# A two-layer diffusion backbone on one Trainium2 core: smaller position table, start normalization per modulation set, output projection in two token parts

## The chip, the cores and the metric

The kernel runs on one core of one Trainium2 chip. The metric is device microseconds of one launch. Five instruction streams matter: PE (TensorE; PEld are its weight loads), DVE (VectorE), ACT (ScalarE), POOL (GpSimd), and SP, which only issues DMAs. Each runs its own list in order and waits for others by semaphores.

## The reference, cut to what matters

640 tokens of 1024 channels go through two layers: 512 latent tokens with a position embedding added, and 128 context tokens. Each group has its own shift, scale and gate, from a small product with `w_mod`.

```python
er = r[:, None] * omega                 # r = t // 64, 8 values
ec = col[:, None] * omega               # col = t % 64, 64 values
pos = concatenate([sin(er), cos(er), sin(ec), cos(ec)], -1)
...
h = rmsnorm(x, norm_g) * (1.0 + scale) + shift
z = h @ w_in                            # feeds three mixers: Hyena, S5, gated DeltaNet
...
merged = sum(gates * proj)              # one projection and gate per mixer
x = x + gate * (merged @ w_out)         # output projection, residual
```

After two layers there is one last `rmsnorm`.

## The kernel before, in words

Activations lie channels on partitions, tokens along the row: `x` is eight tiles `xs[k]` of [128 channels, 640 tokens], tokens 0 to 511 latent, 512 to 639 context. For a float32-like product each operand is split in a high and a low half by `split`: ACT copies the rounded high half (L69), DVE or POOL subtracts for the low half (L70). `mm3` (L91) then makes three matmuls for each of 8 channel blocks. `proj` makes one output tile: two weight pieces of 4 blocks (`kh` 0, 1), each used for token slices 0:320 and 320:640, so 48 matmuls of 320 columns.

`start` loads `x` (tiles `xi`), the full position table (two tiles of 1 MB) and layer 0's modulation weights (four sets `wm`, 2 MB each). It transposes `x` on PE, adds the table (L271), sums squares (`square_acc`), then runs `mod_set` four times. Set `s` gives shift and scale for channel blocks `s` and `4+s`. `norm_h` stands behind all of it: `rstd` becomes a row over all partitions (`dg`, two matmuls with ones L352 and L353, `rs`), and for each of eight blocks `k` it multiplies (`xn`, L359), applies scale and shift (`hf`, L362), and splits into `hh` and `hl`.

Then in each layer: the S5 mixer and Hyena interleaved, the DeltaNet, and `merge`. The 40 gate tiles (`gates`, PSUM name `pg`) are projections that nobody needs until `merge`, 48 matmuls each; in the program they are free to stand between the mixers' own matmuls. `merge` ends with the output projection: for each of eight tiles `i` a full `proj` of all 640 tokens (operands `mh`, `ml`), the gated residual (L132), square and sum (L323, L324). After the last tile come `rstd` (PE L333, DVE `rsv`, POOL L338) and the next layer's `norm_h`, or `final`, which transposes `x` back, scales and stores.

The order of instructions within each engine is not written by hand: a list scheduler with a model of time places them when the program is built, so an edit anywhere can move rows everywhere. Line numbers here are those of the kernel before. In the rows of the changed program most of them are shifted: L90 is the matmul of `mm3`, L131 the residual, L330 and L333 the squares, L334 their sum, L344 to L350 `rstd`, L365 and L366 the ones-matmul and `rs`, L374 `xn`, L378 `hf`, L296 `mrow`.

## Time and profile before

| | |
|---|---|
| median of 3 runs | 3660.12 us (3655.4 to 3660.27) |
| profiled execution, device time | 3638.89 us |
| span of its instructions | 3637.1 us |
| PE busy | 3347.8 us (92%) |
| DVE busy | 2371.0 us (65%) |
| POOL busy | 1948.5 us (54%) |
| ACT busy | 1414.8 us (39%) |
| mean granted TensorE clock | 0.958 |

PE is the engine that is nearly always at work; the other engines have room on the whole, but not in every stage. [...]

### The profile page before, as it was taken

What the parts mean: (1) busy time and instruction counts of PE and PEld (TensorE: products, weight loads), DVE (VectorE), ACT (ScalarE), POOL (GpSimd) and SP (SyncE); (2) the same over time, 40 slices, a digit from 0 to 9 for tenths busy, and PEclk for the clock granted to TensorE, in tenths of its full rate; (3) what the DMA queues carried; (4) which work ended last, traced back from release to release, by engine and by line L of the source; (5) the groups of instructions that cost most, each with busy time, mean ns of one, the idle gap of its engine ahead of it and who ended that gap; (6) DMA issues with size and microseconds to landing.
All of it is one profiled execution on the core that took longest, in us unless ns stands there. A gap on an engine that the chain in (4) does not pass through costs nothing.

```text
span 3637.1 us, 68480 instructions
## 1 busy us (share of the span) xinstructions
PE 3347.8 (92%) x25850; PEld 3198.3 (88%) x25850; DVE 2371.0 (65%) x4615; ACT 1414.8 (39%) x3295; POOL 1948.5 (54%) x2153
## 2 busy tenths in 40 slices
PE   6899988899999999899979999999999999899998
PEld 5898877799899999899968888988898998898998
DVE  5767677667537876743747776677773378875354
ACT  4433322233254556353334333333322545555422
POOL 3887777668545444301336778787774454351010
PEclk7899988899999999999989999999999999899999
DMA  6322334322232222543623222233222322134352
GB/s 238 122 64 77 88 109 140 96 69 78 74 100 75 68 70 86 169 135 112 196 99 101 73 76 85 75 79 81 77 61 74 107 69 77 46 104 166 111 182 87
DMA packets 294195, 363.04 MB, mean 100 GB/s; under 512 B 86792, under 2 KB 169768, under 8 KB 293610
## 3 DMA queue, kind: packets, MB, share of 16 engines
q1 hardware_dynamic: 282050, 342.15, 30.7%
q10 hardware_dynamic: 11816, 16.53, 1.6%
q8 instruction: 204, 3.34, 0.4%
q14 instruction: 125, 1.02, 0.1%
HBM read 291.87 MB, written 66.67 MB: 99 GB/s over the span
## 4 chain that ended last, share of the span: by engine, by line
PE 47%; DVE 18%; POOL 11%; issue 8%; DMA 3%; ACT 2%; SPq 1%; POOLq 0%; DVEq 0%; ACTq 0%
PE pj L91 21%; PE pg L91 10%; DVE lt L1334 2%; DVE Yl L1335 2%; PE pb L129 1%; POOL Y L669 1%; POOL et L830 1%; POOL wl L70 1%; PE pb L659 1%; PE pb L661 1%; POOL E L829 1%; DVE R L939 1%; PE pb L997 1%; PE pb L908 1%; POOL E L831 1%
## 5 line engine op out<-in xcount | busy, mean ns | idle before, releaser
L91 PE MATMUL pj<-hh,wh 128*128 128x320 f32 x2048 | 656.4, 321 | 28.3 <-ACT hh L69 17.6
L91 PE MATMUL pj<-hl,wh 128*128 128x320 f32 x2048 | 652.9, 319 | 5.6 <-DVE hl L70 5.5
L91 PE MATMUL pj<-hh,wl 128*128 128x320 f32 x2048 | 649.9, 318 | 2.4 <-POOL wl L70 2.2
L69 ACT CAST wh<-wr 128x512 fp32r<-128x512 f32 x608 | 374.8, 618 | 662.1 <-PE pj L91 515.2
L70 POOL TENSOR_TENSOR wl<-wr,wh 128x512 fp32r<-128x512 f32 x288 | 394.2, 1372 | 380.9 <-ACT wh L69 340.8
L91 PEld LDWEIGHTS pj<-hh,wh 128*128 128x128 f32 x2048 | 393.4, 192 | 37.0 <-ACT hh L69 19.8
L91 PE MATMUL pg<-hh,wh 128*128 128x320 f32 x1280 | 417.7, 327 | 7.0 <-ACT gst L1423 3.4
L70 DVE TENSOR_TENSOR wl<-wr,wh 128x512 fp32r<-128x512 f32 x320 | 252.5, 791 | 253.9 <-ACT wh L69 252.4
L91 PE MATMUL pg<-hh,wl 128*128 128x320 f32 x1280 | 411.6, 326 | 6.0 <-POOL wl L70 6.0
L91 PE MATMUL pg<-hl,wh 128*128 128x320 f32 x1280 | 412.3, 323 | 0.0
L91 PEld LDWEIGHTS pj<-hl,wh 128*128 128x128 f32 x2048 | 393.1, 192 | 11.1 <-DVE hl L70 8.8
L91 PEld LDWEIGHTS pj<-hh,wl 128*128 128x128 f32 x2048 | 392.4, 192 | 5.9 <-POOL wl L70 3.5
L91 PE MATMUL pj<-yl,wh 128*128 128x320 f32 x1024 | 318.0, 311 | 2.5 <-DVE yl L70 2.2
L91 PE MATMUL pj<-yh,wh 128*128 128x320 f32 x1024 | 317.0, 312 | 2.0 <-ACT yh L69 1.2
L91 PE MATMUL pj<-yh,wl 128*128 128x320 f32 x1024 | 316.9, 310 | 0.0
L91 PEld LDWEIGHTS pg<-hh,wh 128*128 128x128 f32 x1280 | 252.4, 197 | 9.8 <-ACT wh L69 5.3
L91 PEld LDWEIGHTS pg<-hh,wl 128*128 128x128 f32 x1280 | 249.1, 196 | 10.7 <-POOL wl L70 9.2
L91 PEld LDWEIGHTS pg<-hl,wh 128*128 128x128 f32 x1280 | 252.0, 197 | 0.9 <-issue 0.4
L91 PEld LDWEIGHTS pj<-yl,wh 128*128 128x128 f32 x1024 | 193.2, 189 | 4.0 <-DVE yl L70 4.0
L91 PEld LDWEIGHTS pj<-yh,wh 128*128 128x128 f32 x1024 | 192.6, 189 | 3.5 <-ACT yh L69 2.2
L91 PEld LDWEIGHTS pj<-yh,wl 128*128 128x128 f32 x1024 | 193.1, 189 | 0.0
L1513 POOL TENSOR_TENSOR m<-m,gt 128x640 f32<-128x640 f32 x16 | 31.1, 1943 | 294.4 <-DVE gt L132 294.4
(523 smaller groups left out, 8675.9 us busy)
## 6 DMA issues: line engine op xcount, KB each, us to landing
wr<-in_wt SPq DMA_DIRECT2D x608, 256.0 KB, 2.8
gt<-gst SPq DMA_DIRECT2D x160, 160.0 KB, 2.0
gt<-gt SPq DMA_DIRECT2D x64, 320.0 KB, 3.3
wr<-in_wmod SPq DMA_DIRECT2D x64, 256.0 KB, 3.1
Pm<-gcd ACTq DMA_DIRECT2D x32, 320.0 KB, 3.7
wm<-in_wmod SPq DMA_DIRECT2D x4, 2048.0 KB, 18.8
M<-ks SPq DMA_DIRECT2D x256, 32.0 KB, 1.8
us<-u ACTq DMA_DIRECT2D x16, 328.0 KB, 3.2
```

Of the source, the lines that this page charges most:

```text
L69: self.nc.scalar.copy(h, src)
L70: (eng or self.nc.vector).tensor_tensor(l, src, h.bitcast(F32), op=ALU.subtract)
L91: ins = self.nc.tensor.matmul(o, w[:, k, :m], x[:, kh * 4 + k, s], start=kh == 0 and k == 0 and i == 0, stop=kh == 1 and k == 3 and i == 2)
L129: self.nc.tensor.transpose(out, in_, self.ident[:k, :k])
L659: nc.tensor.matmul(pv[:, f, 0, :], D[mr][:, k, j], z[:, k, xr, :], start=k == 0, stop=k == 1)
L661: nc.tensor.matmul(pv[:, f, 1, :], D[mi][:, k, j], z[:, k, xi, :], start=k == 0, stop=k == 1)
L669: nc.gpsimd.tensor_tensor(Y[:, fs, 0, :], p1[:, :nf, 0, :], p2[:, :nf, 0, :], op=ALU.subtract)
L829: nc.gpsimd.tensor_tensor(E[:, 0:2, :, d], E[:, 0:2, :, s], bc(E[:, 0:1, :, e:e + 1], sh), op=ALU.mult)
L830: nc.gpsimd.tensor_tensor(t, E[:, ::-1, :, s], bc(m, sh), op=ALU.mult)
L831: nc.gpsimd.tensor_tensor(E[:, 0:2, :, d], E[:, 0:2, :, d], t, op=ALU.add)
L1334: nc.vector.tensor_tensor(tv, bc(LL[:, c:c + 1, 0:c], sh), bc(Y[:, c:32, c:c + 1], sh), op=ALU.mult)
L1335: nc.vector.tensor_tensor(Y[:, c:32, 0:c], Y[:, c:32, 0:c], tv, op=ALU.subtract)
```

## The change

Four edits. (1) The position table holds 8 row values and 64 column values (288 numbers a partition, 0.15 MB) and is broadcast in the add. (2) In `start` the ones-matmuls and `rs` come before the modulation sets, and after each set the two channel blocks that it serves are normalized; `x` is stored to DRAM last. (3) The output projection runs in two passes, tokens 0:384 and 384:640; each does residual, squares, `rstd` and the next layer's normalization for its tokens. The second weight pieces stay in SBUF from pass one (`kept`, in the memory of the tiles that the projections before just read); the first pieces are loaded and split again. The merged operand moves to other memory (its rows are now named `yh`, `yl`), since `hh`, `hl` are being written for the next layer. (4) Six small loads a layer are issued by SP instead of ACT.

```diff
@@ start
-        with self.pool(name="st", bufs=2) as p:
+        with self.pool(name="nm", bufs=2) as pn, self.pool(name="st", bufs=2) as p:
+            pos = p.tile([128, 288], F32, name="pos", bufs=1)
+            nc.sync.dma_start(pos, a["pos"])
...
-            pos = [p.tile([128, KT // 2, NLAT], F32, name="pos%d" % h, bufs=1) for h in range(2)]
...
-                nc.vector.tensor_tensor(xk[:, :NLAT], ps, pos[k // 4][:, k % 4, :], op=ALU.add)
+                sh = [128, 8, 64]
+                g = bc(row[:, k, :].unsqueeze(2), sh) if k < 4 else bc(col[:, k - 4:k - 3, :], sh)
+                nc.vector.tensor_tensor(xk[:, :NLAT].rearrange("p (r c) -> p r c", r=8),
+                                        ps.rearrange("p (r c) -> p r c", r=8), g, op=ALU.add)
...
-                nc.sync.dma_start(self.xd[0][k], xk)
                 self.xs.append(xk)
+            self.norm_h(0, pn)
             for s in range(4):
                 self.mod_set(0, s, [wm[s][:, k] for k in range(KT)], self.bank(), self.bank(), p)
+                for k in (s, 4 + s):
+                    self.norm_k(0, k, pn)
+            for k in range(KT):
+                nc.sync.dma_start(self.xd[0][k], self.xs[k])
@@ norm_h (dg, ones-matmuls, rs for tokens t0..t1), then
+    def norm_k(self, l, k, p, t0=0, t1=5):
...
+        nc.vector.tensor_tensor(t[:, w], xk[:, w], self.rs[:, w], op=ALU.mult)
+        h = p.tile([128, NTOK], F32, name="hf")
+        for i, (b, e) in enumerate(((w.start, min(w.stop, NLAT)), (NLAT, w.stop))):
+            if e > b:
+                nc.scalar.activation(h[:, b:e], t[:, b:e], AF.Identity, bias=md[:, k, i:i + 1],
+                                     scale=md[:, 8 + k, i:i + 1])
+        self.split(self.hh[:, k, w], self.hl[:, k, w], h[:, w])
@@ hyena, filter_mlp (six loads: alt, hcw, hcb, w1, w2, fb)
-            nc.scalar.dma_start(self.alt, a["alt"])
+            nc.sync.dma_start(self.alt, a["alt"])
...
@@ merge
-        self.pm = P(name="pmo", bufs=1, space=PSUM)
+        self.pm = P(name="pmo", bufs=3, space=PSUM)
...
-            Po = proj(W_OUT + i, (mh, ml))
-            for s, (b, e) in enumerate(((0, NLAT), (NLAT, NTOK))):
-                self.stt(xk[:, b:e], Po[:, b:e], md[:, 16 + i, s:s + 1], xk[:, b:e], ALU.mult, ALU.add)
-            self.square_acc(p, i, xk)
...
+        kept = [py[0].tile([128, KT, 512], F32R, name="w" + x, tag="y" + x) for x in "hl"]
+        for t0, t1 in ((0, 3), (3, 5)):
+            w = slice(t0 * 128, t1 * 128)
+            for i in range(KT):
+                xk = self.xs[i]
+                Po = q[1].tile([128, 1024], F32, name="pj")[:, 0:(t1 - t0) * 128]
+                self.mm3(Po, 0, *self.load_w(l, W_OUT + i, 0, q), mh, ml, w)
+                kw = [x[:, i, :].rearrange("p (k c) -> p k c", k=4) for x in kept]
+                if t0 == 0:
+                    self.load_w(l, W_OUT + i, 1, q, kw)
+                self.mm3(Po, 1, *kw, mh, ml, w)
...
+                self.square_acc(p, i, xk, t0, t1)
...
             if l + 1 < self.depth:
-                nc.sync.dma_start(self.xd[l + 1][i], xk)
+                self.norm_h(l + 1, pn, t0, t1)
+                for k in range(KT):
+                    self.norm_k(l + 1, k, pn, t0, t1)
```

Three places show how the scheduler now places the rows.

On ACT at the start of the program, before the change, the four copies `mrow` (one for each modulation set) come first, then small DMA issues, then `rs` and the normalization:

```order
L289 COPY mrow<-pb 128x128 x4
L692 DMA lr<-in_lr 128x64
L693 DMA li<-in_li 128x64
L695 DMA stp<-in_ls 64x64 x2
L354 COPY rs<-pb 128x512
L697 DMA s_542<-in_s 128x128
L784 DMA sd<-in_sd 128x16
L362 ACTIVATE hf<-xn,mod_91 128x512
L362 ACTIVATE hf<-xn,mod_91 128x128
L69 CAST wh<-wr 128x512 x2
```

After the change, on the same engine at the same place, and further down where the normalization ends:

```order
L366 COPY rs<-pb 128x512
L366 COPY rs<-pb 128x128
L296 COPY mrow<-pb 128x128
L378 ACTIVATE hf<-xn,mod_91 128x512
L378 ACTIVATE hf<-xn,mod_91 128x128
L378 ACTIVATE hf<-xn,mod_91 128x512
L378 ACTIVATE hf<-xn,mod_91 128x128
L69 CAST hh<-hf 128x640
L296 COPY mrow<-pb 128x128
...
L69 CAST hh<-hf 128x640
L802 DMA sd<-in_sd 128x16
L69 CAST wh<-wr 128x512 x6
```

`rs` has moved ahead of the sets, two blocks are normalized behind each `mrow`, and the first weight cast `wh`, which stood behind the first `hf`, now stands behind all eight blocks.

On DVE at the end of layer 0's `merge`, before the change, everything of the norm follows the last residual:

```order
L132 SCALAR_TENSOR_TENSOR x_20601<-pj,mod_91,x_20601 128x512
L132 SCALAR_TENSOR_TENSOR x_20601<-pj,mod_91,x_20601 128x128
...
L324 TENSOR_TENSOR sqs<-sqs,sqt 128x640
L894 TENSOR_TENSOR M_21056<-T_21036,BR 128x512
L138 TENSOR_SCALAR rsv<-pb 128x5
...
L136 TENSOR_SCALAR dg<-c_66,rstd 128x128 x5
L355 COPY rs<-pb 128x128
L359 TENSOR_TENSOR xn<-x_20119,rs 128x640
```

After the change, on DVE in the second pass, the normalization of tokens 0:384 stands among the residuals of tokens 384:640 (two pieces of 128 columns, since latent and context tokens have different gates):

```order
L131 SCALAR_TENSOR_TENSOR x_20118<-pj,mod_91,x_20118 128x128 x2
L334 TENSOR_TENSOR sqs_20544<-sqs_20544,sqt 128x256
L374 TENSOR_TENSOR xn<-x_20116,rs 128x384
L374 TENSOR_TENSOR xn<-x_20117,rs 128x384
L70 TENSOR_TENSOR wl<-wr,wh 128x512
L131 SCALAR_TENSOR_TENSOR x_20119<-pj,mod_91,x_20119 128x128 x2
L374 TENSOR_TENSOR xn<-x_20118,rs 128x384
L374 TENSOR_TENSOR xn<-x_20119,rs 128x384
L70 TENSOR_TENSOR hl<-hf,hh 128x384 x2
```

All eight `xn` and all eight `hl` of 384 columns stand ahead of the last residual; the S5 constants (`M` of L894), which stood between the last residual and `dg`, now come later.

On DVE at the very end of the program, after the change:

```order
L334 TENSOR_TENSOR sqs_40405<-sqs_40405,sqt 128x256
L131 SCALAR_TENSOR_TENSOR x_40041<-pj,mod_96,x_40041 128x128 x2
L334 TENSOR_TENSOR sqs_40405<-sqs_40405,sqt 128x256
L131 SCALAR_TENSOR_TENSOR x_40042<-pj,mod_96,x_40042 128x128 x2
L334 TENSOR_TENSOR sqs_40405<-sqs_40405,sqt 128x256
L137 TENSOR_SCALAR rsv_40662<-pb 128x2
L131 SCALAR_TENSOR_TENSOR yo<-pb,rstd,fg 128x512 x10
```

All ten scalings `yo` of the final norm still stand behind the last `rsv`, as before the change.

## Rows read from the trace of the kernel before

**Rows 1.** Busy time by stage: stretch, length, then each engine's busy us (instructions), clock, DMA:

```profile
54.70:995.40 940.70, 859.74 (x6547) 803.37 (x6548) 659.71 (x1111) 303.30 (x827) 692.54 (x794) 0.94 0.33 93
995.40:1546.60 551.20, 515.63 (x4415) 497.71 (x4412) 363.80 (x943) 284.54 (x627) 253.23 (x265) 0.98 0.29 94
...
1854.50:1895.10 40.60, 18.15 (x66) 13.73 (x67) 27.06 (x35) 19.05 (x41) 24.34 (x30) 0.62 0.14 43
1895.10:2800.80 905.70, 843.88 (x6328) 805.72 (x6327) 631.65 (x957) 296.59 (x801) 669.10 (x762) 0.98 0.29 79
2800.80:3306.60 505.80, 470.65 (x4024) 452.45 (x4022) 350.53 (x931) 268.42 (x591) 236.23 (x251) 0.94 0.28 91
...
3561.00:3618.00 57.00, 57.00 (x389) 56.76 (x387) 22.75 (x36) 13.88 (x21) 0.00 (x0) 1.00 0.18 60
```

**Rows 2.** Timeline of PE at the layer boundary: start us, duration us, what, idle before it:

```profile
1854.18 0.31 PE L91 MATMUL pj<-mh,wl 128*128 128x320 f32 x1
...
1875.88 0.63 PE L91 MATMUL pj<-hh,wh 128*128 128x320 f32 x1 [4.63 <-ACT hh L69]
...
1887.37 0.47 PE L91 MATMUL pj<-hh,wh 128*128 128x320 f32 x1
1887.63 0.47 PE L91 MATMUL pj<-hl,wh 128*128 128x320 f32 x1
...
1895.10 0.33 PE L91 MATMUL pg<-hh,wh 128*128 128x320 f32 x1
```

**Rows 3.** Timeline at the start, ACT, DVE, POOL and PE:

```profile
14.46 2.48 DVE L271 TENSOR_TENSOR x<-pb,pos 128x512 f32<-128x512 f32 x4 [10.42 <-PE pb L129]
...
28.18 1.17 POOL L338 TENSOR_TENSOR rstd<-rsv,c 128x5 f32<-128x5 f32 x1 [27.75 <-DVE rsv L138]
...
31.48 0.27 ACT L289 COPY mrow<-pb 128x128 f32<-128x128 f32 x1 [7.08 <-PE pb L286]
...
54.69 0.63 PE L91 MATMUL pj<-hh,wh 128*128 128x320 f32 x1 [6.78 <-ACT hh L69]
...
74.28 0.47 PE L91 MATMUL pg<-hh,wh 128*128 128x320 f32 x1
```

**Rows 4.** Groups by form, 1810 to 1895 us, DVE and ACT: count, busy us, mean ns:

```profile
L70 DVE TENSOR_TENSOR hl<-hf,hh 128x640 fp32r<-128x640 f32 x8 | 8.6, 1114 | 1.0 <-ACT hh L69 1.0
L132 DVE SCALAR_TENSOR_TENSOR x<-pj,mod,x 128x512 f32<-128x512 f32 x8 | 6.0, 750 | 16.3 <-PE pj L91 16.3
...
L132 DVE SCALAR_TENSOR_TENSOR x<-pj,mod,x 128x128 f32<-128x128 f32 x8 | 2.7, 343 | 0.0
...
L362 ACT ACTIVATE hf<-xn,mod 128x512 f32<-128x512 f32 x8 | 6.5, 814 | 3.1 <-DVE hl L70 2.2 <-DVE xn L359 0.9
L69 ACT CAST hh<-hf 128x640 fp32r<-128x640 f32 x8 | 5.4, 716 | 0.0
...
L362 ACT ACTIVATE hf<-xn,mod 128x128 f32<-128x128 f32 x8 | 3.8, 478 | 0.0
```

**Rows 5.** Timeline of PE in Hyena's filters, matmuls of 256 columns:

```profile
265.96 0.28 PE L530 MATMUL pb<-w3h,hdn 128*128 128x256 f32 x1
266.08 0.28 PE L531 MATMUL pb<-w3l,hdn 128*128 128x256 f32 x1
```

**Rows 6.** Busy time by stage, the first 100 us of each layer's projections:

```profile
54.70:155.00 100.30, 85.57 (x471) 79.30 (x472) 79.08 (x150) 49.73 (x108) 75.62 (x77) 0.82 0.39 127
1875.90:1975.00 99.10, 85.25 (x531) 79.01 (x532) 68.05 (x76) 48.44 (x97) 51.75 (x51) 0.92 0.35 98
```

**Rows 7.** Timeline at the end, DVE and POOL:

```profile
3618.06 1.01 DVE L132 SCALAR_TENSOR_TENSOR x<-pj,mod,x 128x512 f32<-128x512 f32 x2 [4.34 <-PE pj L91]
...
3622.37 1.18 POOL L338 TENSOR_TENSOR rstd<-rsv,c 128x5 f32<-128x5 f32 x1 [112.12 <-DVE rsv L138]
```

**Rows 8.** Line L908 (S5's first use of its layer) in layers 0 and 1: duration min/median/max ns, first and last start:

```profile
L908 PE MATMUL pb<-U,mt x256: 232/275/505, 98.4 to 861.3; 128*128 128x82 f32 x128
...
L908 PE MATMUL pb<-U,mt x256: 232/275/338, 1907.5 to 2659.1; 128*128 128x82 f32 x128
```

More of the change, by code (lines that the diff above doesn't have):

```diff
@@ L255, in start @@
                 nc.sync.dma_start(xi[t], a["x"][t * 128:(t + 1) * 128])
[L256 to L258 removed]
+            row = pos[:, 0:32].rearrange("p (k r) -> p k r", k=4)
+            col = pos[:, 32:288].rearrange("p (k c) -> p k c", k=4)
             wm = []
@@ L324, in square_acc, with rstd_cols @@
             nc.vector.tensor_tensor(self.sq, self.sq, s, op=ALU.add)
         if k == KT - 1:
-            self.rstd_cols(p)
-    def rstd_cols(self, p):
+            self.rstd_cols(p, t0, t1)
+    def rstd_cols(self, p, t0, t1):
         nc = self.nc
+        n = t1 - t0
         ps = self.bank()
-        for t in range(5):
+        for t in range(n):
             nc.tensor.matmul(ps[:, 2 * t:2 * t + 2], self.sq[:, t * 128:(t + 1) * 128], self.ones2,
                              start=True, stop=True)
-        v = p.tile([128, 5], F32, name="rsv")
-        self.ts(nc.vector, v, ps[:, 0:10:2], 1.0 / DM, EPS)
-        self.rstd = self.mp.tile([128, 5], F32, name="rstd", bufs=2)
-        nc.gpsimd.tensor_tensor(self.rstd, v, self.mhalf[:, 0:5], op=ALU.pow)
@@ L340, in norm_h @@
-    def norm_h(self, l):
-        tc, nc = self.tc, self.nc
-        self.hh = self.hp.tile([128, KT, NTOK], F32R, name="hh", tag="hh")
-        self.hl = self.hp.tile([128, KT, NTOK], F32R, name="hl", tag="hl")
-        md = self.mod[l]
-        with self.pool(name="nm", bufs=2) as p:
-            r = self.rstd
-            dg = p.tile([128, 5, 128], F32, name="dg", bufs=1)
-            for t in range(5):
-                self.ts(nc.vector, dg[:, t, :], self.ident, r[:, t:t + 1])
-            rs = p.tile([128, NTOK], F32, name="rs", bufs=1)
-            pa, pb = self.bank(), self.bank()
-            nc.tensor.matmul(pa, self.ones, dg[:, 0:4, :], start=True, stop=True)
-            nc.tensor.matmul(pb[:, :128], self.ones, dg[:, 4, :], start=True, stop=True)
-            nc.scalar.copy(rs[:, :NLAT], pa)
-            nc.vector.tensor_copy(rs[:, NLAT:], pb[:, :128])
-            for k in range(KT):
-                xk = self.xs[k]
-                t = p.tile([128, NTOK], F32, name="xn")
-                nc.vector.tensor_tensor(t, xk, rs, op=ALU.mult)
-                h = p.tile([128, NTOK], F32, name="hf")
-                for i, (s, e) in enumerate(((0, NLAT), (NLAT, NTOK))):
-                    nc.scalar.activation(h[:, s:e], t[:, s:e], AF.Identity, bias=md[:, k, i:i + 1],
-                                         scale=md[:, 8 + k, i:i + 1])
-                self.split(self.hh[:, k, :], self.hl[:, k, :], h)
@@ new lines, in rstd_cols, with norm_h @@
+        v = p.tile([128, n], F32, name="rsv%d" % t0, bufs=1)
+        self.ts(nc.vector, v, ps[:, 0:2 * n:2], 1.0 / DM, EPS)
+        if t0 == 0:
+            self.rstd = self.mp.tile([128, 5], F32, name="rstd", bufs=2)
+        nc.gpsimd.tensor_tensor(self.rstd[:, t0:t1], v, self.mhalf[:, 0:n], op=ALU.pow)
+    def norm_h(self, l, p, t0=0, t1=5):
+        tc, nc = self.tc, self.nc
+        if t0 == 0:
+            self.hh = self.hp.tile([128, KT, NTOK], F32R, name="hh", tag="hh")
+            self.hl = self.hp.tile([128, KT, NTOK], F32R, name="hl", tag="hl")
+            self.dg = p.tile([128, 5, 128], F32, name="dg", bufs=1)
+            self.rs = p.tile([128, NTOK], F32, name="rs", bufs=1)
+        for t in range(t0, t1):
+            self.ts(nc.vector, self.dg[:, t, :], self.ident, self.rstd[:, t:t + 1])
+        for b, e in ((t0, min(t1, 4)), (4, t1)):
+            if e > b:
+                ps = self.bank()[:, :(e - b) * 128]
+                nc.tensor.matmul(ps, self.ones, self.dg[:, b:e, :], start=True, stop=True)
+                nc.scalar.copy(self.rs[:, b * 128:e * 128], ps)
@@ L1501, in merge @@
             self.split(y[0][:, i, :], y[1][:, i, :], t)
-        mh, ml = [self.hp.tile([128, KT, NTOK], F32R, name="m" + x, tag="h" + x) for x in "hl"]
         m = [self.xtile(i, "m") for i in range(KT)]
```

59 lines of the change are left out of this document (36 added, 23 removed).

## The prediction

> **What bounds the kernel now.** I read the busy time by stage first. In the output projection PE has no gap: 389 matmuls in 57.00 us, 0.1465 us each [rows 1]. In the S5-and-Hyena stages it is busy 859.7 of 940.7 us in layer 0 and 843.9 of 905.7 in layer 1, in DeltaNet 515.6 of 551.2 and 470.7 of 505.8 [rows 1]. The two DeltaNet stages make a natural experiment: layer 1 has less PE work there (45.0 us less busy) and is 45.4 us shorter [rows 1]. So that stage goes at PE's pace, and projections that are done earlier, as gates are, come off it nearly one for one.
>
> What is left to gain is time in which PE has nothing. The stage from 1854.5 to 1895.1 is the worst: 40.6 us with 66 matmul records and a granted clock of 0.62 [rows 1]. The PE timeline shows it: the last output projection starts at 1854.18, the next layer's first projection at 1875.88, and that projection's 48 matmuls end only where the first gate begins, at 1895.10 [rows 2]. [...] The start is alike: first projection 54.69, first gate 74.28 [rows 3]. The end is a third such place, residual at 3618.06, then a serial tail to the span's end at 3637.1 [rows 7].
>
> **The change part by part.**
>
> *Start.* The old table came late: the first add stands at 14.46 though transposes had been going [rows 3]. With 0.15 MB in place of 2 MB I take 2.5 us off the squares, so POOL's `rstd` (28.18 + 1.17 [rows 3]) ends near 26.9; `dg`, two ones-matmuls and `rs` end near 31. PE makes these ahead of the modulation sets now, so the first set's `mrow` (31.48 [rows 3]) moves back to about 34, and its shift and scale are ready near 35.6. From there ACT sets the pace: one block costs one `hf` pair and one `hh`, 0.81 + 0.48 + 0.72 = 2.0 us [rows 4], 1.9 with what overlaps; eight are 15.3 us, three more `mrow` 0.8. So the normalization ends at 51.7. The first `wh` stands behind it on ACT (rows in the section on the change), so PE begins at 52.5, hardly before the 54.69 of today. But then all operands are there: 48 matmuls at 0.26 us are 12.5 us, so the first gate starts at 65 in place of 74.28 [rows 3]: **9 us**. Bounds: 14, if the clock comes back at once (48 at 0.1465); 4, if the small loads that ACT still issues among the blocks hold it for 5 us.
>
> *Output projection.* The count of matmuls stays, 320 + 320 columns become 384 + 256. Two of 256 start 0.12 us apart [rows 5], one of 320 takes 0.1465 [rows 1]; the line through both gives 0.173 for 384, and 0.173 + 0.12 is 0.293, as twice 0.1465. So no PE time is lost; a row for 384 does not exist, and a loss of 5% there would be 1.7 us a layer. Eight more weight pieces are loaded and split in the second pass, half the rate of today's projections, hidden behind 23 us of matmuls.
>
> New is a wait at the head of the first pass. `kept` lies in memory that the last mixer's projection still reads, so its split can only start when that ends; and the last merged tile goes through four DVE and ACT instructions that today are covered by a 48-matmul `proj`. Now only about 3.6 us of matmuls (12 of the first piece, 9 of the second) cover them. I take 1.5 us in each layer: **3 us lost** (0 to 6).
>
> *Layer boundary.* In the second pass DVE has eight residual pairs, sums, `xn` and `hl`. A residual takes 750 ns for 512 columns and 343 for 128 [rows 4], that is 0.21 us and 1.06 ns a column. So 256 columns are 0.48 and 384 are 0.61 us, and the pass holds 8 x (0.69 + 0.48 + 0.61 + 0.61) + 2 for weights = 21 us in 23 us of PE. The order puts all of `xn` and `hl` for the first part ahead of the last residual, and they can't begin before `rs` of that part, some 11 us into the pass. I take a slip of 2 us (0 to 5). [...]
>
> Behind the last residual the tail for 256 tokens is: pair 0.6, square 0.4, sum 0.5, two matmuls and `rsv` 1.0, POOL 1.2 [rows 7], `dg` 0.5, ones-matmuls 1.2, `rs` 0.6, `xn` 0.5, `hf` pair and `hh` 1.2, handoffs 0.5: about 8 us. Before, POOL and DVE also put S5's constants between; the first projection came 21.7 us after the last output matmul [rows 2]. Then ACT brings one block in 1.15 us (two `hf` of 128 columns, `hh` of 256), with five `wh` 12 us in all, and PE at half clock needs 12.5 for its 48. So the first projection ends 2 + 8 + 13 = 23 us behind the last output matmul, 40.6 before: **17 us gained** (10 to 25).
>
> *What is given back there.* Before, S5's constants of layer 1 were computed during the output projection; now they come behind the boundary, as they always do in layer 0. The first 100 us of the two layers price it: 471 matmul records in layer 0, 531 in layer 1 [rows 6]; 60 x 0.1465 is 8.8 us. Part of that belongs to the start's own slow normalization and lower clock, so I take **4 us lost** (0 to 9).
>
> *End.* In the order all ten `yo` stay behind the last `rsv`, so nothing of the final norm overlaps with the second pass. Only the chain is shorter: from the residual to POOL's start is 4.3 us [rows 7], with 256 columns and two matmuls about 2.5. **2 us gained** (1 to 4).
>
> *Small loads* from ACT to SP: 0.3 to 0.6 us of issue each on an engine that is not late; nothing. If SP were late there, a layer's first weights would wait for them, under 3 us.
>
> Sum: -9 + 3 - 17 + 4 - 2 = **-21 us**. On the profiled execution, 3638.89 us of device time, that is 3618. The three runs have a median of 3660.12, 0.6% above the profiled one; I carry the difference over: **3639 us**. Runs of this kernel spread by 0.13%, so 0.2% is about what can be told from no change.
>
> **The rivals.**
>
> *It is larger.* If S5's constants stay covered, the clock returns early and no slip occurs, the lower ends give -14 - 25 - 4 = -43: 3617. For it: layer 1 of the changed order has 272 projection and gate rows ahead of S5's first use, 127 before, which can cover the constants. Against it: ACT and DVE are both nearly full in the second pass.
>
> *The gain is lost further on.* S5's chain, not PE, may set the pace of its stage. The scheduler puts 160 more gate rows in layer 0 and 80 more in layer 1 ahead of DeltaNet; if they fill what was idle, the gain is kept, if they only sit in front of the chain it is not. For it: PE has 81 and 62 us of idle time in those stages, POOL 692 and 669 us of work [rows 1]. Against it: the DeltaNet pair above. If half of the 26 us of start and boundary stays lost, the sum is -8 and less: 3652 to 3660, about the same.
>
> *Slower.* The same mechanism in full, at one place, the first use of S5's layer (PE is in order, and more rows stand ahead of it). Layer 0: 98.4 [rows 8], 53 + 42 + 6 (half clock) = 101 after. Layer 1: 53 us behind the boundary (1907.5 [rows 8] less 1854.5), 2 + 8 + 39 + 6 = 55 after. If the rest of each stage hangs on that moment, the two layers lose 2.5 + 2, the passes 3, the end gives 2, and the 240 gate rows (35 us) come off DeltaNet only by some nine tenths, 4 lost: +9, 3669. It decides from the point at which the whole gain of 26 is hidden behind that chain.
>
> A slip of the second pass on DVE can't decide by itself: its 5 us leave -18.
>
> **How the numbers follow.** Forecast 0.68, larger gain 0.10, lost further on 0.11, slower 0.11. The likeliest case alone spans 3622 to 3652. The range takes in the larger gain (3617, and some for a schedule that differs in every stage) and the lower part of the slower rival: 3611 to 3662, with about 2 in 10 outside. Faster by over 0.2% (below 3652.8): 0.78; same 0.11; slower 0.11.
>
> **What would show it.** Right: first gate near 65; the boundary stage about 23 us from the last 256-column matmul to the first gate of layer 1; `hl` of 384 columns inside the second pass; POOL's last `rstd` 2.5 us after the last residual; DeltaNet stages shorter by the gates moved. Wrong: the first gate still behind 70, or matmuls of 384 columns above 0.18 us; PE idle over 4 us at the head of a first pass; the S5-and-Hyena stages longer by more than the 23 and 12 us of gates that they take over.

## The result, and the profile after

The changed kernel takes 3684.09 us (median of 4 runs) where the kernel before takes 3657.76 in the same series: ratio 1.0072, interval 1.0055 to 1.0089, 26 us slower. The forecast was 21 us faster. The two profiled executions differ by 50 us of span (3637.1 and 3687.4), since before's is faster than all its timed runs and after's is the slowest. So the stages below are set against a second profile of the unchanged kernel, same_again (span 3645.9), which lies at the median of its runs. These come from another series, in which the kernel before has a median of 3648.46 and not 3657.76; so the stages below add up to 41.5 us, more than the ratio's 26.

Busy time by stage of the changed kernel, answering [rows 1]: stretch, length, busy us of PE, PEld, DVE, ACT, POOL (instructions), clock, DMA share, GB/s. The clock is the granted TensorE clock as a share of its highest level: in 2-us steps up to 3636 us it reads 1.00 in 1626 of 1818 and 0.50, the lowest, in 109, so a value between is in general a mixture over the stretch. The stretches are layer 0 (S5 and Hyena, DeltaNet, the merge's other projections, output projection), the boundary, and the same for layer 1.

```profile
67.90:1008.70 940.80, 860.79 (x6660) 801.99 (x6659) 658.24 (x1097) 297.62 (x819) 690.28 (x799) 0.96 0.34 94
1008.70:1572.30 563.60, 519.39 (x4373) 496.75 (x4371) 382.15 (x1000) 295.12 (x667) 247.81 (x261) 0.95 0.29 93
1572.30:1803.50 231.20, 229.50 (x1538) 228.40 (x1537) 100.48 (x132) 78.09 (x104) 15.55 (x8) 0.98 0.45 142
1803.50:1868.30 64.80, 60.65 (x394) 60.06 (x392) 39.56 (x79) 29.00 (x54) 0.86 (x1) 0.95 0.33 111
1868.30:1888.90 20.60, 11.82 (x58) 10.03 (x57) 13.66 (x42) 11.09 (x29) 15.51 (x10) 0.83 0.44 133
1888.90:2831.10 942.20, 863.37 (x6413) 822.06 (x6413) 655.60 (x1040) 308.01 (x837) 717.19 (x809) 0.97 0.31 81
2831.10:3378.90 547.80, 488.15 (x4101) 462.56 (x4098) 376.31 (x1000) 288.85 (x646) 232.08 (x249) 0.93 0.27 86
```

The boundary did what was foreseen: 40.6 us became 20.6. But the output projection is longer, and layer 1's stage with the DeltaNet takes 547.8 us with PE at work for only 488.15: 60 us idle, where before had 35 [rows 1].

PE's timeline at the boundary, answering [rows 2]. `pj<-hh` is the first projection of layer 1, `pg` the first gate:

```profile
1872.00 0.61 PE L344 MATMUL pb<-c,sqs 128*128 128x2 f32 x4 [3.45 <-DVE sqs L334]
...
1876.10 0.63 PE L90 MATMUL pj<-hh,wh 128*128 128x320 f32 x1 [0.87 <-ACT wh L69]
...
1880.94 0.42 PE L90 MATMUL pj<-hh,wh 128*128 128x320 f32 x1
1882.65 0.42 PE L90 MATMUL pg<-hh,wh 128*128 128x320 f32 x1 [1.29 <-ACT wh L69]
...
1883.34 0.30 PE L90 MATMUL pj<-hl,wh 128*128 128x320 f32 x1
...
1889.02 0.31 PE L90 MATMUL pg<-hh,wh 128*128 128x320 f32 x1
```

The last output matmul starts at 1868.27, so the first gate comes 14.4 us behind it, 40.9 before. That is not equal work. Before, all 48 matmuls of the first projection stand ahead of the first gate; here 19 do (the last is the one at 1880.94), and the projection goes on behind four gate matmuls. Counted by work, the 48th projection or gate matmul starts 20.8 us behind the last output matmul (at 1889.02) and 40.8 in same_again: the boundary gained 20 us.

The start, answering [rows 3], from the timelines of DVE, POOL, ACT and PE:

```profile
11.94 0.69 DVE L273 TENSOR_TENSOR x<-pb,pos 128x512 f32<-128x512 f32 x1 [7.94 <-PE pb L128]
...
27.43 1.17 POOL L350 TENSOR_TENSOR rstd<-rsv,c 128x5 f32<-128x5 f32 x1 [27.00 <-DMA wm<-in_wmod]
...
34.80 0.27 ACT L296 COPY mrow<-pb 128x128 f32<-128x128 f32 x1 [2.13 <-PE pb L293]
...
57.31 0.64 PE L90 MATMUL pj<-hh,wh 128*128 128x320 f32 x1 [6.11 <-ACT wh L69]
...
67.92 0.31 PE L90 MATMUL pg<-hh,wh 128*128 128x320 f32 x1
```

The first add is 2.5 us earlier, as put, but `rstd` gains only 0.8. The first `mrow` is 3.3 us later and the first projection 2.6; the first gate is 6.4 us earlier.

For all kernels below, stage lengths read in the same way, from PE's timeline: first gate of layer 0; then up to DeltaNet's first matmul (S5+Hy); up to the first output matmul (DN+merge); the output projection (out); its last matmul to layer 1's first gate (bound.); the same for layer 1; the rest to PE's last matmul.

| kernel | gate 0 | S5+Hy 0 | DN+merge 0 | out 0 | bound. | S5+Hy 1 | DN+merge 1 | out 1 | rest |
|---|---|---|---|---|---|---|---|---|---|
| same_again | 74.4 | 920.1 | 804.7 | 57.5 | 41.3 | 908.3 | 764.1 | 56.2 | 12.3 |
| changed kernel | 67.9 | 940.8 | 794.7 | 64.8 | 14.4 | 948.5 | 777.4 | 61.2 | 10.7 |
| before_psum3 | 73.7 | 923.7 | 814.9 | 57.5 | 40.8 | 914.2 | 785.2 | 56.2 | 12.2 |
| after_psum1 | 67.0 | 938.7 | 784.3 | 63.1 | 14.4 | 947.4 | 756.4 | 59.7 | 10.3 |
| two_pass_psum1 | 74.2 | 921.6 | 804.5 | 61.8 | 11.4 | 939.4 | 760.8 | 59.5 | 10.4 |
| start_only | 67.7 | 939.6 | 797.2 | 57.5 | 40.9 | 911.7 | 772.5 | 56.2 | 13.0 |
| null_edit | 74.5 | 924.0 | 807.3 | 58.1 | 40.9 | 908.7 | 772.9 | 56.2 | 12.2 |
| table_only | 68.7 | 931.7 | 811.9 | 57.5 | 43.6 | 922.6 | 772.6 | 56.2 | 12.3 |
| no_kept | 67.5 | 941.1 | 783.6 | 58.4 | 20.1 | 926.4 | 780.0 | 57.8 | 10.5 |
| early_constants | 74.4 | 919.3 | 802.5 | 65.2 | 17.5 | 943.1 | 758.7 | 57.5 | 10.2 |

Three things have to be kept in mind with this table. "bound." ends at the first gate, so it is not equal work either: the 48th projection or gate matmul stands 40.8 us behind the last output matmul in same_again, 20.7 in after_psum1, 20.6 in two_pass_psum1, 27.8 in no_kept and 25.4 in early_constants. S5+Hy holds different numbers of gate matmuls (`pg`): 1610 and 1442 in same_again (layers 0 and 1), 1770 and 1522 in the changed kernel, and in layer 1 1564 in after_psum1, 1538 in two_pass_psum1 and early_constants, 1379 in no_kept. And two profiles differ by themselves: in layer 0 null_edit has the rows of same_again in the same order on every engine, and its S5+Hy 0 and DN+merge 0 are 3.9 and 2.6 us longer. A difference under some 4 us in one stage says nothing.

Between same_again and the changed kernel the first gate of layer 1 comes 26.9 us sooner (20 by equal work, the other 7 lie behind the gate, in S5+Hy), the start gives 6.5, and the output projections take 7.3 and 5.0. S5+Hy grows by 20.7 and 40.2, of which the 160 and 80 gate rows moved ahead of DeltaNet account for 23.4 and 11.7 at 0.1465 us. DN+merge should have shrunk by as much; it goes by -10.0 and +13.3.

### The profile page after: what moved, and what is told of

The parts are those of the page before. It is cut to its first block, busy times and chain, and to the rows that moved or that the text cites. A ratio compares the mean times of both kernels' runs of the same rounds, so it can differ in the third digit from the quotient of the medians.

```text
span 3687.4 us, 68703 instructions
## 1 busy us (share of the span) xinstructions
PE 3362.5 (91%) x25852; PEld 3203.3 (87%) x25852; DVE 2401.0 (65%) x4677; ACT 1434.6 (39%) x3349; POOL 1950.2 (53%) x2155
## 4 chain that ended last, share of the span: by engine, by line
PE 34%; DVE 13%; POOL 6%; DMA 4%; issue 4%; ACT 2%; SPq 1%; ACTq 0%; DVEq 0%; POOLq 0%
PE pj L90 19%; PE pg L90 6%; DVE lt L1352 2%; DVE Yl L1353 2%; DMA wr<-in_wt 1%; POOL wl L70 1%; DVE wl L70 1%; PE pb L128 1%; DVE R L957 1%; DMA U<-us 1%; POOL Y L687 1%; DMA gt<-gt 1%; PE pb L926 1%; DMA out_ns_out<-fs 1%; DVE N L131 0%
## 5 line engine op out<-in xcount | busy, mean ns | idle before, releaser
L69 ACT CAST wh<-wr 128x512 fp32r<-128x512 f32 x624 | 383.6, 618 | 684.0 <-PE pj L90 473.7
L70 DVE TENSOR_TENSOR wl<-wr,wh 128x512 fp32r<-128x512 f32 x336 | 274.9, 821 | 252.4 <-ACT wh L69 246.5
L90 PE MATMUL pg<-hh,wl 128*128 128x320 f32 x1280 | 406.4, 321 | 17.6 <-POOL wl L70 17.5
L90 PE MATMUL pj<-yh,wh 128*128 128x320 f32 (+2 forms) x1280 | 399.2, 312 | 9.4 <-DVE x L131 6.4
L90 PE MATMUL pj<-yl,wh 128*128 128x320 f32 (+2 forms) x1280 | 399.2, 312 | 1.1 <-DVE yl L70 0.9
L90 PE MATMUL pj<-yh,wl 128*128 128x320 f32 (+2 forms) x1280 | 398.6, 312 | 0.0
L90 PEld LDWEIGHTS pg<-hh,wh 128*128 128x128 f32 x1280 | 249.3, 195 | 19.9 <-ACT wh L69 10.6
L90 PEld LDWEIGHTS pj<-yh,wh 128*128 128x128 f32 x1280 | 243.3, 190 | 10.7 <-DVE x L131 7.1
L90 PEld LDWEIGHTS pj<-yl,wh 128*128 128x128 f32 x1280 | 243.3, 190 | 2.2 <-DVE yl L70 2.2
L90 PEld LDWEIGHTS pj<-yh,wl 128*128 128x128 f32 x1280 | 243.3, 190 | 0.1
```

The costliest lines, as they stand in the source:

```text
L69: self.nc.scalar.copy(h, src)
L70: (eng or self.nc.vector).tensor_tensor(l, src, h.bitcast(F32), op=ALU.subtract)
L90: ins = self.nc.tensor.matmul(o, w[:, k, :m], x[:, kh * 4 + k, s], start=kh == 0 and k == 0 and i == 0, stop=kh == 1 and k == 3 and i == 2)
```

## The experiments

**The parts alone.** Each is the kernel before with one part of the change.

start_only: edits (1) and (2), with before's merge and queues.

```diff
+            pos = p.tile([128, 288], F32, name="pos", bufs=1)
...
+            self.norm_h(0, pn)
...
+                for k in (s, 4 + s):
+                    self.norm_k(0, k, pn)
```

> The kernel before with the start of the changed one alone (position table of 0.15 MB, norm per modulation set); its output projection, its layer boundary and the queue of the small loads stay as before, and so does the order of layer 1. By the sum of the prediction: -9 us, some 3649 where the kernel before takes 3658. By the theory that the S5 chain and not PE sets the end of the first stages, so that what PE has sooner is given back behind it: the gain of about 6 us at the first gate is gone by the first DeltaNet stage, 0 to +7 us in all, 3658 to 3665.

two_pass_only: edit (3) with all of its pools, before's start and queues.

```diff
+        for t0, t1 in ((0, 3), (3, 5)):
...
+                self.norm_h(l + 1, pn, t0, t1)
+                for k in range(KT):
+                    self.norm_k(l + 1, k, pn, t0, t1)
```

> The kernel before with the output projection in two parts alone, the next layer's normalization per part; start, small loads and the order of layer 0 up to its output projection stay as before. By the sum of the prediction: +3 at the heads, -17 at the boundary, +4 for late constants, -2 at the end, -12 us, some 3646. By the theory that layer 1 gives it back (constants and chain of S5 come later in it, and the heads of the passes cost 7 us each): +14 - 20 + 25 to 50 - 1, that is +18 to +40 us, 3676 to 3698, nearly the whole loss of the changed kernel.

queue_only:

```diff
-            nc.scalar.dma_start(self.alt, a["alt"])
+            nc.sync.dma_start(self.alt, a["alt"])
... (hcw, hcb, w1, w2, fb likewise)
```

> The kernel before with its six small loads of S5 and Hyena's stage issued by SP in place of ACT, nothing else. By the prediction: nothing, within 4 us of before (3654 to 3662). By the rival that these loads now stand behind weights and transform tables and hold up Hyena's start: +5 to +15 us, and the time shows in the first 100 us of either layer.

merged_home:

```diff
-        mh, ml = [self.hp.tile([128, KT, NTOK], F32R, name="m" + x, tag="h" + x) for x in "hl"]
...
                 y = self.load_y(pl, self.ytile(py[0]), self.yd[2], 32)
+                mh, ml = self.ytile(py[1])
```

> The kernel before with only the home of the merged tiles changed: mh and ml lie in the memory of the second mixer's tiles (as in the changed kernel), which the constants of layer 1's S5 used to take over early. One output projection of 640 columns, normalization behind it as before. By the theory that this home is what makes layer 1's constants late: +10 to +25 us, and DVE's constants of layer 1 stand behind the last residual in the trace. By the rival that their lateness is harmless, because the projections ahead of S5's first use cover it: within 5 us of before.

Measured: start_only 1.0040 (1.0027 to 1.0052), two_pass_only 1.0133 (1.0120 to 1.0147), queue_only 1.0026 (1.0016 to 1.0037), merged_home 1.0046 (1.0032 to 1.0060). No part gains, and alone they lose more than together (+14, +47, +9 us against +26). merged_home is no part of its own; it costs 15 us and has them at the boundary, 60.9 us in place of 41.3: layer 1's constants now stand there, `rstd` starts behind a power of 10.77 us on POOL, and PE waits 13.47 us for `dg`. Its S5+Hy 1, with 52 gate matmuls fewer, is 13.4 us shorter, its DN+merge 1 8.3 longer. two_pass_only goes beyond even the theory that layer 1 gives it back, and its trace shows something that no theory had: layer 0, whose order is untouched up to DeltaNet's end, had DN+merge at 813.7 in place of 804.7. The first projection of the merge starts only behind DeltaNet's last matmul there. In the program's order of TensorE DeltaNet's last matmul stands 149 and 168 rows behind the merge's first one in the kernel before (the merge's own rows among them, here and where the expectations count them), and ahead of it in two_pass_only. One line of the diff moves PSUM: `pmo`.

**The PSUM pool.**

```diff
-        self.pm = P(name="pmo", bufs=3, space=PSUM)
+        self.pm = P(name="pmo", bufs=1, space=PSUM)
```

This on the changed kernel is after_psum1, on two_pass_only two_pass_psum1; the reverse on the kernel before is before_psum3. same_again is the kernel before, unedited.

> The changed kernel with one line as before: the merge's pool of small PSUM banks has 1 buffer and not 3, so the pair of projection banks behind it lies where it lay before. By the theory that those two banks take the merge's first projections away from the end of DeltaNet (with 3, none of the merge's projections stands ahead of DeltaNet's last matmul, with 1 some 193 of DeltaNet's stand behind the first one): the idle time of PE at the end of both DeltaNet stages goes, 12 to 20 us a layer, 3644 to 3660 where the changed kernel has 3684 and the kernel before 3651 to 3658. By the rival that the loss lies in S5's late constants and chain alone: within 6 us of the changed kernel.

> The kernel before with that line alone as in the changed kernel: 3 buffers in place of 1 (the two more are not used by anything). By the theory of the banks: +12 to +20 us a layer, 3675 to 3690. By the rival: nothing, within 4 us of before.

> The two-part output projection alone on the kernel before, with 1 buffer in that pool. What is left of two_pass_only's +47 us is the projection itself with its boundary and the late constants of S5. By the theory of the banks: 25 to 35 us come back, +12 to +22 against before. If the boundary's gain is then kept in full as the prediction had it: -10 us. By the rival: still +40 us or more.

> The kernel before once more, unchanged, for a second profile of it: its first one was faster than all its timed runs. Each theory expects a ratio of 1.000; the profile should be some 12 us longer than the first one, and shows in which stages such executions differ (by the profiles of start_only and queue_only: in S5 and Hyena and in the merge of layer 1).

Measured: after_psum1 1.0012 (1.0002 to 1.0023), before_psum3 1.0105 (1.0087 to 1.0123), two_pass_psum1 1.0021 (1.0010 to 1.0031), same_again 0.9997 (0.9988 to 1.0007). The theory of the banks holds, and the rival is out: two banks that nothing uses cost the kernel before 38 us, and by its profile 31 of 39 lie in DN+merge (10.2 and 21.1). Busy time in steps of 20 us at the end of layer 0's DeltaNet, the changed kernel first:

```profile
1500.00:1520.00 20.00, 14.71 (x156) 14.01 (x156) 12.59 (x35) 9.93 (x20) 5.82 (x5) 0.83 0.69 223
1520.00:1540.00 20.00, 15.14 (x223) 13.55 (x221) 10.83 (x22) 10.51 (x25) 0.00 (x0) 0.88 0.55 190
1540.00:1560.00 20.00, 17.92 (x115) 16.04 (x115) 13.42 (x43) 9.00 (x23) 0.00 (x0) 0.86 0.22 67
1560.00:1580.00 20.00, 15.74 (x88) 14.08 (x88) 7.82 (x26) 8.48 (x34) 2.33 (x2) 0.83 0.30 97
```

The same stretch of same_again:

```profile
1500.00:1520.00 20.00, 18.30 (x282) 17.11 (x281) 15.14 (x34) 9.34 (x21) 5.26 (x4) 1.00 0.81 295
1520.00:1540.00 20.00, 20.00 (x191) 19.48 (x190) 7.36 (x19) 4.78 (x11) 5.15 (x4) 1.00 0.24 76
1540.00:1560.00 20.00, 18.97 (x136) 17.95 (x135) 11.17 (x25) 10.51 (x23) 0.00 (x0) 1.00 0.34 103
1560.00:1580.00 20.00, 18.05 (x130) 16.74 (x128) 11.50 (x37) 9.41 (x30) 0.00 (x0) 1.00 0.31 105
```

DeltaNet's last scan is a chain of small matmuls between which PE waits for DVE or ACT: in these 80 us of the changed kernel 6.0 us for DVE's `os` and `r` and 4.2 for ACT's `Z` and `vn`, and gates 5.3 more for DVE's `gst`. What fills the waits is the merge's first two projections, and these need `pjm`'s two double banks. Allocated behind a `pmo` of 3, those banks lie, by the theory, where DeltaNet still works; what the orders show is that in all three kernels with 3 buffers the merge's first projection stands behind DeltaNet's last matmul, in all with 1 ahead of it. Without filler PE idles 16.5 of these 80 us (4.7 in same_again), and the granted clock falls to 0.83 to 0.88, a mixture of its two levels: the matmuls that are there go slower too. In the changed kernel gate matmuls of 320 columns start 0.27 us apart from 1509 to 1514 us, behind a wait of 3.66 us for `gst`, and the clock reads 0.50; from 1515 to 1516.5 they start 0.147 apart, and it reads 1.00.

With the banks back the changed kernel is still 4 us slower, where 21 faster was forecast.

**Without the kept weights, and the parts again.** First the edit of no_kept, on after_psum1; two_pass_no_kept is two_pass_psum1 with this edit and the small table. loads_on_act is after_psum1 without edit (4), table_only the kernel before with edit (1) alone.

```diff
-                if t0 == 0:
-                    self.load_w(l, W_OUT + i, 1, q, kw)
-                self.mm3(Po, 1, *kw, mh, ml, w)
+                self.mm3(Po, 1, *self.load_w(l, W_OUT + i, 1, q), mh, ml, w)
```

> after_psum1 (the changed kernel with 1 buffer in the merge's small PSUM pool) without the kept weights: the second pass loads and splits both halves of each weight tile, so the memory of the first mixer's tiles is free as soon as the last mixer's projections end. The program then puts the constants of layer 1's S5 between the first part's normalization and the second's, no longer behind both. By the theory that late constants cost layer 1 some 14 us (merged_home) and that the head of the first pass waits for that memory (5.6 and 3.5 us by the profile of after_psum1): 10 to 20 us faster than after_psum1, 3632 to 3642 against 3648 before. By the rival that VectorE and ScalarE are full in the second pass, with 32 more split instructions there: no faster than after_psum1, 3652 to 3660.

```diff
-            nc.sync.dma_start(self.alt, a["alt"])
+            nc.scalar.dma_start(self.alt, a["alt"])
```

> after_psum1 with the six small loads back on ScalarE's queue. By the theory that this move cost its 9 us (queue_only) only by another order at the end of layer 1's DeltaNet, and nothing by the loads themselves: within 6 us of after_psum1, 3646 to 3658. By the rival that the loads hold Hyena up behind the weights on SP's queue: 8 us or more faster.

```diff
+            pos = p.tile([128, 288], F32, name="pos", bufs=1)
+            nc.sync.dma_start(pos, a["pos"])
```

> The kernel before with the small position table alone: the norm stays whole and behind the modulation sets. By the prediction's own term for the table: first add some 2.5 us earlier, the first gate 0 to 2 us earlier, the whole within 2 us of before as far as this part goes. By the theory that any edit which reorders the end of layer 1's DeltaNet costs what start_only and queue_only lost there (193 of its matmuls behind the merge's first projection, where before has 168): +6 to +10 us, 3654 to 3658.

> The kernel before with the small table and the two-part output projection, 1 buffer in the small PSUM pool, and no kept weights; norm per set and the move of the loads left out. By the theories so far (start per set gives nothing back in layer 0, constants of layer 1 early, no wait at the heads): boundary -27, S5 and Hyena of layer 1 longer by 12 to 20 beyond the gates moved, heads 0: 5 to 15 us faster than before, 3633 to 3643. By the rival that VectorE is full in the second pass: about the same as two_pass_psum1, 3650 to 3658.

Measured: no_kept 1.0004 (0.9994 to 1.0013), loads_on_act 1.0027 (1.0017 to 1.0037), table_only 1.0109 (1.0094 to 1.0124), two_pass_no_kept 1.0059 (1.0047 to 1.0071). no_kept gives back the wait at the heads (out 58.4 and 57.8) and is the best two-part version, level with the kernel before; its other term, an earlier first use of the constants, did not come (S5's first matmul 63.1 us behind the last output matmul, 59.8 in after_psum1). loads_on_act came out 4 to 5 us slower than after_psum1, so the loads themselves hold nothing up. table_only was the surprise: it brings 5.7 of the start's 7 us and then loses 44, in S5+Hy (11.6 and 14.3), DN+merge (7.2 and 8.5) and the boundary (2.3). No expectation had that. two_pass_no_kept, which has its order of TensorE in layer 0, has the loss there too (932.0 and 809.9), so it belongs to the program and not to one execution; whether to this order or to the small table with the old norm, which both have, no run tells apart.

**S5's first use.** By then the theory was that each S5-and-Hyena stage ends a fixed time behind S5's first use (`U,mt`), which comes late when its constants do. Their chain begins with loads and two powers on POOL. The timeline of POOL in the changed kernel, layer 0 and, in the last two rows, layer 1:

```profile
56.68 10.70 POOL L716 TENSOR_TENSOR stp<-c,stp 128x64 f32<-128x64 f32 x1 [21.14 <-DMA stp<-in_ls]
69.86 10.54 POOL L721 TENSOR_TENSOR smag<-c,smag 128x64 f32<-128x64 f32 x1
...
1873.55 10.54 POOL L716 TENSOR_TENSOR stp<-c,stp 128x64 f32<-128x64 f32 x1
1888.53 10.55 POOL L721 TENSOR_TENSOR smag<-c,smag 128x64 f32<-128x64 f32 x1 [1.77 <-DVE smag L719]
```

In the kernel before the first power of layer 0 starts at 49.38 and that of layer 1 at 1748.24, during the merge. s5_powers_both computes them ahead, into two tiles of 64 columns (s5_powers_layer1 for layer 1 only, both on after_psum1; before_powers on the kernel before):

```diff
+    def s5_powers(self, l):
+        st, mag = self.spow = [self.mp.tile([128, 64], F32, name=n) for n in ("pst", "pmag")]
...
+        nc.gpsimd.tensor_tensor(st, self.ebase[:, 0:64], st, op=ALU.pow)
+        nc.vector.tensor_tensor(mag, mag, st, op=ALU.mult)
+        nc.gpsimd.tensor_tensor(mag, self.ebase[:, 0:64], mag, op=ALU.pow)
```

null_edit writes one memset of layer 1's constants 8 times:

```diff
-        nc.vector.memset(PR[:, 0, :], 1.0)
+        for _ in range(8 if l == 1 else 1):
+            nc.vector.memset(PR[:, 0, :], 1.0)
```

> after_psum1 with the two powers of S5's constants (10.6 us each on GpSimd) taken out of the chain in both layers: for layer 0 they are computed at the very start from loads of their own, for layer 1 inside layer 0's DeltaNet; two tiles of 64 columns keep them. By the theory that each S5-and-Hyena stage hangs on S5's first use: that use comes some 19 us earlier in layer 0 and 13 to 15 in layer 1 (then the path over the projection and DRAM bounds it), and the whole is 20 to 34 us faster than after_psum1, 3618 to 3632, faster than before. By the rival that the loss lies at the end of DeltaNet or in PE's own work: within 8 us of after_psum1.

> The same for layer 1 alone. By the theory: S5's first use in layer 1 some 45 us behind the last output matmul in place of 60, 8 to 15 us faster than after_psum1, 3637 to 3644. By the rival: within 6 us of it.

> The kernel before with the powers taken out in both layers, nothing else of the change. By the theory: in layer 0 S5's first use some 10 us earlier, in layer 1 unchanged, since there the constants were computed during the output projection: 5 to 10 us faster, 3638 to 3643, if the end of DeltaNet does not take it (8 us). By the rival: within 4 us of before or slower.

> The kernel before with one memset of 64 columns written 8 times in layer 1's constants, under 1 us of VectorE where it is not late. The order of TensorE is the same as before up to the end of layer 1's DeltaNet; there the merge's first projection stands 193 DeltaNet matmuls ahead of the last one where before has 168. By the theory that this order alone costs what start_only and queue_only lost in layer 1: +6 to +10 us, 3653 to 3657. By the rival that those losses had causes of their own: within 3 us of before.

Measured: s5_powers_both 1.0120 (1.0104 to 1.0136), s5_powers_layer1 1.0014 (1.0005 to 1.0023), before_powers 1.0022 (1.0013 to 1.0031), null_edit 1.0031 (1.0019 to 1.0043). The theory failed: in s5_powers_both S5's first use came at 92.8 us (108.7 in after_psum1) and the stage ended at 1029.8 (1005.7). Part of it is the edit's own doing: on POOL the two powers now stood ahead of `rstd`, 36.53 us in before_powers where same_again has 28.67, and the first gate slipped to 84.1 there. In s5_powers_layer1 the first use of layer 1 came 54.6 us behind the last output matmul (59.8 in after_psum1), and boundary and S5+Hy 1 together took 964.9 us (961.8) with 42 gate matmuls fewer. Its layer 0 was 15 us shorter than after_psum1's (last output matmul at 1838.1 and 1853.1), though no power of that layer had moved, and layer 1 gave it back.

null_edit cost 12 us, a little more than expected. TensorE's order is that of the kernel before until past the middle of layer 1's DeltaNet (3074 us). From there on rows move, gate matmuls above all, and at the end the merge's first projection stands 25 rows earlier (193 rows ahead of DeltaNet's last, 168 before). Its busy time there, in steps of 20 us:

```profile
3290.00:3310.00 20.00, 14.71 (x93) 14.22 (x93) 14.95 (x46) 10.53 (x27) 6.80 (x5) 0.91 0.67 217
3310.00:3330.00 20.00, 18.29 (x329) 16.46 (x328) 11.17 (x21) 10.93 (x24) 1.28 (x1) 1.00 0.67 223
3330.00:3350.00 20.00, 17.59 (x125) 16.44 (x124) 10.01 (x24) 10.85 (x24) 0.00 (x0) 1.00 0.40 126
```

And same_again, as far into its DeltaNet:

```profile
3282.70:3302.70 20.00, 17.55 (x277) 16.17 (x276) 16.70 (x44) 13.42 (x26) 5.60 (x5) 1.00 1.00 342
3302.70:3322.70 20.00, 18.88 (x176) 17.33 (x175) 9.72 (x23) 8.06 (x18) 0.71 (x1) 1.00 0.27 84
3322.70:3342.70 20.00, 19.29 (x142) 18.37 (x140) 12.12 (x33) 9.76 (x22) 0.00 (x0) 1.00 0.41 129
```

PE is 5 us less busy in those 60, and DN+merge 1 is 8.8 us longer (772.9 and 764.1). start_only has nearly this order there and 772.5 us; queue_only has the 193 rows too, with its gate matmuls elsewhere, and 774.4. Neither edit touches layer 1's DeltaNet, so layer 1's part of their loss goes with the order. The number of rows is no price by itself. start_only and queue_only have 193 rows in layer 0 as well, and no clear loss there: 797.2 and 794.0 us, or 806.6 and 803.1 with the 64 and 62 gate matmuls that went to S5+Hy, against 804.7. before_powers has the first projection 45 rows earlier in layer 1, and 764.0.

**Early constants with the two-part projection.** early_constants on two_pass_psum1, early_constants_full on after_psum1, both with no_kept's edit:

```diff
-                y = self.load_y(pl, self.ytile(py[0]), self.yd[2], 32)
-                mh, ml = self.ytile(py[1])
+                y = [self.hp.tile([128, KT, NTOK], F32R, name="z" + x, tag="h" + x) for x in "hl"]
+                self.load_y(pl, y, self.yd[2], 32)
+                mh, ml = self.ytile(py[0])
```

> two_pass_psum1 (two-part output projection on the kernel before, 1 buffer in the small PSUM pool) with other homes in the merge: the last mixer's tiles lie where the layer's normalized input lay, the merged tiles where the first mixer's lay, and the weights are loaded again in the second pass, so that one 41-KB home is free before the output projection and layer 1's S5 constants are computed ahead of the normalization, as before the change. By the theory that layer 1's stage hangs on S5's first use: that use some 40 us behind the last output matmul (59 in two_pass_psum1), 10 to 18 us faster than it, 3630 to 3643 where before takes 3647 and two_pass_psum1 3652. By the rival: within 6 us of two_pass_psum1, or slower.

> The same homes in after_psum1, that is with the changed start and the moved loads. By the theory: 10 to 18 us faster than after_psum1, 3632 to 3642. By the rival: within 6 us of after_psum1 (3652).

Measured: 1.0033 (1.0021 to 1.0045) and 1.0033 (1.0020 to 1.0046). The rows at S5's first use in layer 1, two_pass_psum1:

```profile
1920.72 1.47 PE L922 MATMUL pb<-U,mt 128*128 128x82 f32 x8
```

early_constants:

```profile
1910.02 1.01 PE L922 MATMUL pb<-U,mt 128*128 128x82 f32 x8
```

That is 58.7 and 48.6 us behind the last output matmul, but boundary and S5+Hy 1 together are 950.8 and 960.6. The first use came 10 us earlier and the stage ended 10 us later, with as many gate matmuls. early_constants_full against after_psum1 is alike: 47.8 and 59.8, 963.1 and 961.8. So the theory fell in both layers: that stage's end does not hang on S5's first use. On when PE gets its projections it may hang in part: two_pass_psum1's 950.8 us hold 96 gate matmuls (14.1 us) more than same_again's 949.6, so by equal work they are 13 us shorter, of 20 gained at the boundary.

No version beats the kernel before; no_kept and after_psum1 come nearest.

## Why the prediction was wrong

**The step that failed.** "The change part by part" gave no term to the pool of small PSUM banks, 1 to 3 buffers, although the diff shows it. By ratios it is worth 22 us (1.0072 to 1.0012, two series), 38 (before_psum3) and 41 (two_pass_only to two_pass_psum1); by the profiles of the changed kernel (its slowest run) and after_psum1, 31 of 39 us lie in DN+merge (10.4 and 21.0). Without it the change is about as fast as the kernel before. It also broke the step "projections that are done earlier, as gates are, come off it nearly one for one": that stage keeps PE's pace only while filler is left, and the banks took the last of it.

**What else the sum had wrong**, after_psum1 against same_again by stage (2.6 us longer by span):

| term | predicted | measured | from |
|---|---|---|---|
| start | -9 | -7.4 | gate 0 |
| layer 0, S5+Hy and DN+merge | 0 | -1.8 | +18.6, -20.4 |
| passes | +3 | +9.1 | out 0, out 1 |
| boundary and S5+Hy 1, less 122 gate rows (17.9 us) | -13 | -5.7 | -26.9 + 39.1 - 17.9 |
| DN+merge 1, with these rows added back | 0 | +10.2 | -7.7 + 17.9 |
| end | -2 | -2.0 | rest |

*Start*: right in size, not in its working. PE began at 57.31 where 52.5 was put, and its 48 matmuls took 10.6 us where 12.5 were, at the 0.26 us each of [rows 2]. The normalization took 20 us on ACT and not 16, and 5.7 us of the gain come with the table alone (table_only). The norm per set adds little, as ACT is in order: `hf` of a set waits 1.2 to 2.5 us for shift and scale, and the next `mrow` stands behind it (PE waited 2.05 and 2.57 us for two of them). The gain was kept in layer 0, where gates did come off DeltaNet: 23.4 us of rows moved, 20.4 us shorter.

*Passes*: 1.5 us each were 5.6 and 3.5. In the changed kernel PE stood still in the first pass for over 4 us, which the prediction named as a sign, though not at the head but 12.8 us into the pass:

```profile
1804.74 0.34 PE L90 MATMUL pj<-yl,wh 128*128 128x384 f32 x1
1804.92 0.34 PE L90 MATMUL pj<-yh,wl 128*128 128x384 f32 x1
...
1816.28 0.69 PE L90 MATMUL pj<-yh,wh 128*128 128x384 f32 x1 [4.16 <-DVE x L131]
```

That residual (1815.61 us) stood on DVE behind low halves of weights, for which DVE had waited 1.91 and 2.31 us; ACT's `wh` ahead of them had waited 1.97 and 2.39 us for the DMA of `wr`. no_kept has 0.9 and 1.6 us there, so `kept`'s memory brings most of it in this program. It is not the only way to it: early_constants has no `kept` and 7.7 us in layer 0. The pace of 384 columns was right: 0.18 us.

*Boundary*: the mechanism was right, and so was the size. The table's 26.9 us are by the first gate; by equal work, 48 matmuls, the prediction put 23 us behind the last output matmul and 20.8 came, 20 us gained where 17 were put. (ACT's 1.15 us a block is low by its own rows: two `hf` of 0.478 and two fifths of 0.716 are 1.24, under 1 us in all.) DVE did not slip: all `hl` of the first part ended before the last residual. DVE's groups by form, 1835 to 1895 us:

```profile
L131 DVE SCALAR_TENSOR_TENSOR x<-pj,mod,x 128x128 f32<-128x128 f32 x16 | 4.9, 346 | 2.0 <-PE pj L90 2.0
L70 DVE TENSOR_TENSOR hl<-hf,hh 128x384 fp32r<-128x384 f32 x8 | 4.3, 550 | 0.0
...
L70 DVE TENSOR_TENSOR hl<-hf,hh 128x256 fp32r<-128x256 f32 x8 | 3.2, 418 | 1.5 <-ACT hh L69 1.5
```

550 ns for 384 columns and 418 for 256 put the fixed part of such an instruction at 0.15 us; the prediction's 0.21 was read from residuals, another instruction, with an operand in PSUM. What makes the two differ no run tells apart.

*What is given back*: 4 us were put for late constants. The first use was indeed late, by 6 us, but making it early bought nothing. Boundary and S5+Hy 1 together took 949.6 us in same_again and 950.8 (two_pass_psum1), 961.8 (after_psum1), 960.6 (early_constants) and 946.5 (no_kept) in the two-part kernels with 1 PSUM buffer tabled here. Less the gate matmuls that they hold beyond same_again's (96, 122, 96 and -63, at 0.1465 us) these are 936.7, 943.9, 946.5 and 955.7. So of 20, 20, 15 and 13 us gained at the front by equal work, 13, 6 and 3 are kept at the stage's end, and no_kept loses 6. Why that stage gives back so much is not settled; the theory of S5's first use fell.

*DN+merge 1*: +10.2 is about null_edit's 8.8. Shown is that an edit without work of its own can bring an order of rows there that costs so much; that after_psum1's 10.2 has this cause is argued from the size.

*End*: right.

**The rivals.** "The gain is lost further on" is what happened to most of the boundary's; whether for its reason, S5's chain, stays open. "Slower" had the sign, by a mechanism (S5's first use) that the runs did not bear out. No rival spoke of an idle tail of DeltaNet. The range, 3611 to 3662, left out that an edit to a scheduled program can cost something before it does anything: null_edit +12 us, and table_only +40, whose cause stays open.

## What to carry to other kernels

Look in a diff for pool sizes first: a buffer more in one pool can move the pools behind it, and what it takes away may be another stage's filler; compare in both programs which work stands between the last links of a chain. Before a gain of 1% is argued from local terms, price a null edit: here a reordered tail cost 12 us, half of what was to be gained. A gain at the head of a stage is kept only if the stage's end moves in a trial; a shorter boundary is no proof. And measure it by equal work: 26.9 us by the first gate were 20 by matmuls done.
